# Linear attention in a fused block: all pairs of token tiles scored, or scores within a tile and states passed between tiles

## Chip, cores and metric

The kernel runs on one core of one Trainium2 chip. Its time is the device time of one execution in microseconds (us), given as the median of several runs. Engines: TensorE (PE) multiplies, VectorE (DVE) and ScalarE (ACT) do elementwise work and read PSUM, GpSimd (POOL) does elementwise work in SBUF, SyncE (SP) issues most DMAs.

## What is computed

One block of a hybrid model on 512 tokens with 1024 features: a joint input projection, a gated linear attention in two directions (4 heads, key width 128, value width 256), a softmax attention with latent keys (8 heads), their gated merge, and a squared-ReLU MLP of width 4096. The part that matters here is the linear attention. With q, k, v of a head and a log decay per token and key feature in each direction:

```python
b = jnp.cumsum(log_a, axis=3)                 # within a chunk
q_dec, k_dec = q * jnp.exp(b), k * jnp.exp(-b)
k_end = k * jnp.exp(b_last - b)
scores = jnp.where(mask, jnp.einsum('bhnck,bhnsk->bhncs', q_dec, k_dec), 0.0)
o_intra = jnp.einsum('bhncs,bhnsv->bhncv', scores, v)
def step(state, inp):                         # from chunk to chunk
    o = jnp.einsum('bhck,bhkv->bhcv', qc, state)
    state = state * dc[..., None] + jnp.einsum('bhck,bhcv->bhkv', kc, vc)
    return state, o
```

The forward direction includes a token's own key, the backward one does not; the two outputs are added, normalised per head, and gated. Everything is in float32; nearly all products are done as three "rounded" products (mm3, L87): each operand is split into a high part, rounded to the fp32r format, and the remainder, and high x high, high x low and low x high are added in PSUM. split (L92) makes the two parts: ACT copies the high one, DVE (or POOL, where given) subtracts for the low one. split_scaled (L96) does it with a scale.

## The kernel before, in words

Tokens lie in four tiles of 128. All activations are kept transposed (features on partitions, 512 tokens in the free dimension). The kernel goes through these stages: the first projections while x lands; the gates and values of the linear attention for all heads by a seven-product scheme (class Seven); the four heads of the linear attention; the softmax attention; the output projection; the MLP.

A head h of the linear attention goes through these steps, with their lines:

- Gates(h) (L435): two products for the log gates, Abs and Exp on ACT; logs (L453) takes the logarithm; sums (L456) does four scans on DVE and one subtraction per direction; exps (L472) makes from them the factors per token (ee) and per tile (e3: decay from a tile's start to its middle, from its middle to its end, and over the tile).
- gla_qk (L486): queries and keys times their factors relative to the middle of their own tile (near, on DVE), and from these on POOL a second pair for neighbouring tiles (nxt) and a third for tiles of the other half (far), each with coefficients multiplied from e3.
- gla_scores (L529): the backward scores within the tiles (bd), and for each key tile j three float32 products that together cover all 512 queries: own tile (L544), neighbour (L545), the two tiles of the other half (L546). The backward half of the diagonal block is put in by a masked copy on DVE (L550). Each [128, 512] result is split.
- gla_out (L701): for each query tile four mm3 of 256 value columns, one per key tile: 48 products.
- gla_squares (L716), gla_gated (L726), gla_turn (L733): the norm's sums on ACT and POOL, the gating on DVE, and four transpositions for each of two value halves.

Between these steps stand projections of 128 output features, each 24 products of 512 columns: za(2h) and za(2h+1) (gates of the merge), gq and gk (queries and keys of head h + 2), and in head 2 the latent projections ckv and cq instead. begin (L235 and L231) loads the 512 KB of weights into one of three staging buffers (tag wf) and splits them into one of four pairs (wh, wl); proj_run (L247) multiplies. begin_late returns the low half's subtraction as a function (lows) that is called later.

Order: PE takes the instructions in program order from the gates on up to the end of head 2 (in_program_order, L1214), ACT and DVE too (L1213). In the last head and the softmax attention a scheduler orders them by readiness and priority, with a few hand-set constraints (goes_behind, L125). PSUM has eight banks in two groups of four: "mm" for projections, gates and turns, "at" for scores and outputs. SBUF buffers are shared by size (29 of one row of 512 floats, u2; 26 of two, u4). The loop over heads 0 to 2 is at L1180; head 3 is interleaved with the latent projections and the rotary products from L1216 to L1262.

Of the kernel before, what the change touches and what calls it, by code (L numbers as in the profile page):

```python
# [18 lines left out]
P = 128  # L19
# [37 lines left out]
def tile_block(ctx: ExitStack, tc: tile.TileContext, t, out: bass.AP):  # L57
# [29 lines left out]
    def mm3(acc, lh, ll, rh, rl, start, stop, onto=False):  # L87
        nc.tensor.matmul(acc, lh, rh, start=start, stop=False, skip_group_check=onto)  # L88
        nc.tensor.matmul(acc, lh, rl, start=False, stop=False, skip_group_check=onto)  # L89
        nc.tensor.matmul(acc, ll, rh, start=False, stop=stop, skip_group_check=onto)  # L90

    def split(hi, lo, src, rest=nc.vector):  # L92
        nc.scalar.activation(hi, src, AF.Copy)  # L93
        rest.tensor_tensor(lo, src, raw(hi), op=ALU.subtract)  # L94
# [140 lines left out]
    def begin_late(col, name, tag="mm", w=None):  # L235

        wf = stage(KD, P, name)
        nc.sync.dma_start(wf, (w_in if w is None else w)[:, col : col + P].rearrange("(k p) w -> p k w", p=P))
        wh, wl = halves(KD, P, name)
        nc.scalar.activation(wh, wf, AF.Copy)  # L240

        def lows():
            nc.vector.tensor_tensor(wl, wf, raw(wh), op=ALU.subtract)

        return (wh, wl, ps(tag, name)), lows
# [237 lines left out]
            nc.scalar.activation(e3, v3, AF.Exp, scale=INV_NORM)  # L483
            self.parts[d] = ee, e3

    def gla_qk(h, parts):  # L486
        near = {}
        for d in ("f", "b"):
            near[d] = u4(f"qk{d}", F32, (P, 2, NT, P))
        for x in range(2):  # L490
            n = qk.pop((h, x))
            for d in ("f", "b"):
                nc.vector.tensor_tensor(
                    near[d][:, x].rearrange("p a b -> p (a b)"), n,
                    parts[d][0][:, x].rearrange("p a b -> p (a b)"), op=ALU.mult,
                )
        nxt = u4("qk2", F32, (P, 2, NT, P))
        far = u4("qk3", F32, (P, 2, NT, P))

        def times(dst, src, coef):  # L500
            nc.gpsimd.tensor_tensor(dst, src, coef.unsqueeze(2).to_broadcast([P, 2, P]), op=ALU.mult)

        cf = {}
        for d in ("f", "b"):
            e3 = parts[d][1]
            fq, fk = (e3[:, 0], e3[:, 1]) if d == "f" else (e3[:, 1], e3[:, 0])
            eT = e3[:, 2]
            odd, even = slice(1, 4, 2), slice(0, 4, 2)
            qs, ks = (odd, even) if d == "f" else (even, odd)
            times(nxt[:, 0, qs], near[d][:, 0, qs], fq[:, qs])  # L510
            times(nxt[:, 1, ks], near[d][:, 1, ks], fk[:, ks])
            c3 = tl([P, 2, NT], F32, "c3", 4, f"c3{d}")
            lo, hi = slice(0, 2), slice(2, 4)
            qs, ks = (hi, lo) if d == "f" else (lo, hi)
            if d == "f":
                nc.gpsimd.tensor_copy(c3[:, 0, 2:3], fq[:, 2:3])
                nc.gpsimd.tensor_tensor(c3[:, 0, 3:4], fq[:, 3:4], eT[:, 2:3], op=ALU.mult)
                nc.gpsimd.tensor_tensor(c3[:, 1, 0:1], fk[:, 0:1], eT[:, 1:2], op=ALU.mult)
                nc.gpsimd.tensor_copy(c3[:, 1, 1:2], fk[:, 1:2])
            else:  # L520
                nc.gpsimd.tensor_tensor(c3[:, 0, 0:1], fq[:, 0:1], eT[:, 1:2], op=ALU.mult)
                nc.gpsimd.tensor_copy(c3[:, 0, 1:2], fq[:, 1:2])
                nc.gpsimd.tensor_copy(c3[:, 1, 2:3], fk[:, 2:3])
                nc.gpsimd.tensor_tensor(c3[:, 1, 3:4], fk[:, 3:4], eT[:, 2:3], op=ALU.mult)
            times(far[:, 0, qs], near[d][:, 0, qs], c3[:, 0, qs])
            times(far[:, 1, ks], near[d][:, 1, ks], c3[:, 1, ks])
        return near, nxt, far

    def gla_scores(near, nxt, far):  # L529
        bd = ps("at", "bd")  # L530
        for j in range(NT):
            nc.tensor.matmul(
                bd[:, j * P : (j + 1) * P], near["b"][:, 1, j], near["b"][:, 0, j], start=True, stop=True
            )
        bds = u2("bds")
        nc.scalar.activation(bds, bd, AF.Copy)
        res = []
        for j in range(NT):
            sc = ps("at", f"sc{j}")
            dj = slice(j * P, (j + 1) * P)  # L540
            n = j + 1 if j % 2 == 0 else j - 1
            far_q = slice(2, 4) if j < 2 else slice(0, 2)
            far_c = slice(2 * P, 4 * P) if j < 2 else slice(0, 2 * P)
            nc.tensor.matmul(sc[:, dj], near["f"][:, 1, j], near["f"][:, 0, j], start=True, stop=True)  # L544
            nc.tensor.matmul(sc[:, n * P : (n + 1) * P], nxt[:, 1, j], nxt[:, 0, n], start=True, stop=True)  # L545
            nc.tensor.matmul(  # L546
                sc[:, far_c], far[:, 1, j], far[:, 0, far_q].rearrange("p a b -> p (a b)"),
                start=True, stop=True,
            )
            nc.vector.copy_predicated(sc[:, dj], after.bitcast(I32), bds[:, dj])  # L550
            hl = u4(f"sc{j}")
            split(hl[:, 0, :], hl[:, 1, :], sc)
            res.append(hl)
        return res

# [145 lines left out]
    def gla_out(h, sc):  # L701

        half, at = h // 2, (h % 2) * GDV
        accs = [ps("at", f"gla{h}o{j}") for j in range(2)]
        c = slice(at, at + GDV)
        os = []
        for i in range(NT):
            o = accs[i // 2][:, (i % 2) * GDV : (i % 2 + 1) * GDV]
            tok = slice(i * P, (i + 1) * P)
            for j in range(NT):  # L710
                mm3(o, sc[j][:, 0, tok], sc[j][:, 1, tok], v[j, half][:, 0, c], v[j, half][:, 1, c],
                    j == 0, j == NT - 1)
            os.append(o)
        return os

    def gla_squares(h, os):  # L716
        tot = sm(f"gla{h}ss")
# [373 lines left out]
    def begin_za(f):  # L1091
        return begin(C_ZA + f * P, f"za{f}")
# [74 lines left out]
    gate.exps("b")  # L1167
    gv.multiply(3)
    gv.multiply(7)
    near, nxt, far = gla_qk(0, gate.parts)  # L1170
    gv.right_split(4, 1)
    w_b = begin(C_ZB + 5 * P, "zb5")
    gv.sinks(3)
# [3 lines left out]
    w_a = begin_za(0)  # L1177
    finish_zb(5, w_b)
    ckv_, cq_ = Latent(C_CKV, 2, V_KV, "ckv"), Latent(C_CQ, 3, V_Q, "cq")
    for h in range(GH - 1):  # L1180
        sc = gla_scores(near, nxt, far)
        gate = Gates(h + 1)
        gate.logs()
        w_b = begin_za(2 * h + 1)
        acc = proj_run(w_a, xT)
        if h < 2:
            w_a, lows = begin_late(C_GQ + (h + 2) * P, f"gq{h + 2}")
        else:
            ckv_.begun[0], lows = begin_late(C_CKV, "ckv0")
        gate.sums("f")  # L1190
        gate.exps("f")
        lows()
        gate.sums("b")
        gate.exps("b")
        za_gate(2 * h, acc)
        os = gla_out(h, sc)
        near, nxt, far = gla_qk(h + 1, gate.parts)
        rs = gla_squares(h, os)
        za_gate(2 * h + 1, proj_run(w_b, xT))
        if h < 2:  # L1200
            w_b = begin_qk(h + 2, 1)
            gla_gated(h, os, rs)
            finish_qk(h + 2, 0, w_a)
            w_a = begin_za(2 * h + 2)
            finish_qk(h + 2, 1, w_b)
        else:
            ckv_.begin(1)
            gla_gated(h, os, rs)
            ckv_.run(0)
            cq_.begin(0)  # L1210
            ckv_.run(1)
        gla_turn(h)
# [17 lines left out]
    cq_.sums()  # L1230
    zb = proj_T(C_ZB + 6 * P, "zb6")
    projected = traced()
    sc = gla_scores(near, nxt, far)
# [5 lines left out]
    goes_behind((at, traced()), (projected, scored), PE_ONLY)  # L1239
    spreading = traced()  # L1240
    cq = cq_.normed()
    goes_behind((spreading, traced()), (projected, scored), PE_ONLY)
# [10 lines left out]
    for _ in range(3):  # L1253
        next(units)
    at = traced()
    os = gla_out(h, sc)
    values = traced()
    for _ in units:
        pass
# [413 lines left out]
```

## Time and profile before

| | us |
|---|---|
| median of 3 runs | 766.08 |
| lowest, highest | 764.56, 766.45 |
| span of the profiled execution, first to last instruction | 764.1 |
| stretch of heads 0, 1, 2 (PE starts of the scores or turns: 144.69, 177.36, 210.76, 244.17) | 32.7, 33.4, 33.4 |
| PE busy in 144.69 to 244.17 | all of it |
| DVE, ACT, POOL busy in 177.36 to 210.76 | 21.4, 19.4, 13.0 |

The profiled execution has no time of its own beside its span; the runs' times include some 2 us around the span. The profile gives, for each instruction, its engine, its line in the kernel, its start and duration, and what ended the idle time before it. Matmul durations overlap, so the distance of their starts is what one costs in a row. Where a helper such as mm3 or split records the operation, the line is the helper's (L88 to L90, L93, L94) and the tile's name tells what it is: sc for scores, gla0o for the output of head 0, za, gq, gk for projections. PEld is the load of the stationary operand, which runs beside the matmuls.

### The profile page before, as it was taken

The numbers are of one execution on the slowest core, as the hardware profiler recorded it, in microseconds if no ns is written. First come the engines' busy times: TensorE is split into PE (matmuls) and PEld (weight loads), VectorE is DVE, ScalarE is ACT, GpSimd is POOL, SyncE is SP. The second block draws the span as 40 slices with busy tenths as digits, with TensorE's granted clock in tenths as the row PEclk, the third lists the DMA queues.
The fourth block names the chain that finished last, engine by engine and source line by source line (L and its number), as shares of the span: only waits on it lengthen the run. The fifth ranks groups of instructions, "written<-read, shape, count | busy, mean of one in ns | idle before, by whom it ended". The sixth has DMA issues, their size and how long they took to land.

```text
span 764.1 us, 10232 instructions
## 1 busy us (share of the span) xinstructions
PE 754.0 (99%) x3744; PEld 637.5 (83%) x3744; DVE 580.7 (76%) x851; ACT 453.1 (59%) x768; POOL 151.1 (20%) x226
## 2 busy tenths in 40 slices
PE   8999999999999999999999999999999999999996
PEld 7888788888898888899888988888888888888885
DVE  7689999765667865898897886965787578748795
ACT  7556658384566555888866775435653555346634
POOL 1630004351605104117762100000000000000014
PEclk9999999999999999999999999999999999999999
DMA  9832411222323516127989421363116410650002
GB/s 317 248 88 88 135 28 28 56 56 56 83 55 91 102 37 155 25 60 187 258 200 242 138 83 55 111 190 86 55 56 190 140 36 21 194 164 1 27 1 110
DMA packets 97073, 81.28 MB, mean 106 GB/s; under 512 B 15376, under 2 KB 74784, under 8 KB 97024
## 3 DMA queue, kind: packets, MB, share of 16 engines
q1 hardware_dynamic: 93760, 74.07, 33.0%
q0 software_dynamic: 2976, 6.05, 4.3%
q8 instruction: 29, 0.48, 0.3%
q10 hardware_dynamic: 288, 0.52, 0.2%
q14 instruction: 20, 0.16, 0.1%
HBM read 76.96 MB, written 2.10 MB: 103 GB/s over the span
## 4 chain that ended last, share of the span: by engine, by line
PE 96%; DVE 1%; ACT 1%; DMA 1%; issue 0%; POOL 0%; POOLq 0%; ACTq 0%
PE f L88 8%; PE f L90 8%; PE f L89 8%; PE gx L88 4%; PE gx L89 4%; PE gx L90 4%; PE first L329 3%; PE tp L1046 2%; PE za L88 2%; PE za L89 2%; PE za L90 2%; PE gz L90 2%; PE gz L88 2%; PE gz L89 2%; PE zb L88 1%; PE zb L89 1%
## 5 line engine op out<-in xcount | busy, mean ns | idle before, releaser
L1612 POOL DMA_DIRECT2D gfin<-in_g_final x1 | 0.6, 622 | 284.0 <-PE f L90 284.0
L918 DVE TENSOR_TENSOR w<-w,w 128x1024 f32<-128x1024 f32 x32 | 38.8, 1223 | 0.3
L479 POOL COPY v3f<-rrf 128x4 f32<-128x4 f32 x4 | 2.8, 707 | 136.0 <-DVE rrf L462 136.0
L1031 ACT ACTIVATE e<-s,top 128x512 f32<-128x512 f32 x32 | 21.9, 685 | 4.7 <-DVE top L1026 3.8
L94 DVE TENSOR_TENSOR pT<-tp,pT 128x512 fp32r<-128x512 f32 x32 | 21.7, 683 | 3.0 <-ACT pT L93 3.0
L1026 DVE TENSOR_REDUCE top<-s 128x1 f32<-128x512 f32 x32 | 21.7, 683 | 2.0 <-PE s L90 1.7
L1339 DVE TENSOR_TENSOR h<-h,gx 128x512 f32<-128x512 f32 x32 | 21.5, 684 | 1.9 <-PE gx L90 1.8
L93 ACT ACTIVATE pT<-tp 128x512 fp32r<-128x512 f32 x32 | 18.8, 592 | 4.3 <-PE tp L1046 4.0
L1046 PE MATMUL tp<-ident,e 128*128 128x128 f32 x128 | 19.3, 274 | 0.4 <-ACT e L1037 0.2
L88 PE MATMUL av<-pT,v 128*128 128x256 f32 x64 | 19.0, 297 | 0.0
L1405 ACT ACTIVATE fa<-f 128x512 f32<-128x512 f32 x32 | 18.5, 577 | 0.0
L93 ACT ACTIVATE ghb<-y 128x512 fp32r<-128x512 f32 x16 | 10.1, 632 | 14.0 <-DVE y L864 14.0
L89 PE MATMUL av<-pT,v 128*128 128x256 f32 x64 | 18.2, 285 | 0.0
L90 PE MATMUL av<-pT,v 128*128 128x256 f32 x64 | 18.2, 284 | 0.0
L1046 PEld LDWEIGHTS tp<-ident,e 128*128 128x128 f32 x128 | 15.1, 140 | 3.7 <-ACT e L1037 1.0
L94 DVE TENSOR_TENSOR sc<-sc,sc 128x512 fp32r<-128x512 f32 x16 | 10.9, 691 | 9.5 <-ACT sc L93 9.5
L93 ACT ACTIVATE sc<-sc 128x512 fp32r<-128x512 f32 x16 | 9.3, 595 | 11.5 <-DVE sc L550 11.5
L93 ACT ACTIVATE b_00h<-w 128x1024 fp32r<-128x1024 f32 x7 | 7.4, 1059 | 12.5 <-PE gx L90 6.0
L93 ACT ACTIVATE b_10h<-w 128x1024 fp32r<-128x1024 f32 x7 | 7.4, 1060 | 12.1 <-PE gx L90 6.0
L93 ACT ACTIVATE b_20h<-w 128x1024 fp32r<-128x1024 f32 x7 | 7.4, 1060 | 12.1 <-PE gx L90 6.0
L88 PE MATMUL s<-kbuf,q 96*128 96x512 f32 x32 | 14.1, 441 | 0.0
L1414 ACT ACTIVATE px<-fa 128x256 f32<-128x256 f32 x32 | 13.4, 418 | 1.0
(1668 smaller groups left out, 2932.2 us busy)
## 6 DMA issues: line engine op xcount, KB each, us to landing
w<-in_w_ff SPq DMA_DIRECT2D x64, 256.0 KB, 3.4
w<-in_w_out POOLq DMA_DIRECT2D x10, 512.0 KB, 9.4
grw<-in_w_in SPq DMA_DIRECT2D x8, 512.0 KB, 9.0
gvw<-in_w_in SPq DMA_DIRECT2D x8, 512.0 KB, 4.9
w<-in_w_out SPq DMA_DIRECT2D x16, 256.0 KB, 5.5
x<-in_xt SPq DMA_DIRECT2D x8, 256.0 KB, 5.3
h<-in_x SPq DMA_DIRECT2D x4, 512.0 KB, 5.0
vw<-in_w_first SPq DMA_DIRECT2D x7, 256.0 KB, 5.4
```

What stands on the lines that cost most here:

```text
L88: nc.tensor.matmul(acc, lh, rh, start=start, stop=False, skip_group_check=onto)
L89: nc.tensor.matmul(acc, lh, rl, start=False, stop=False, skip_group_check=onto)
L90: nc.tensor.matmul(acc, ll, rh, start=False, stop=stop, skip_group_check=onto)
L93: nc.scalar.activation(hi, src, AF.Copy)
L94: rest.tensor_tensor(lo, src, raw(hi), op=ALU.subtract)
L329: nc.tensor.matmul(f_accs[i], a[:, i * P : (i + 1) * P], b, start=k == 0 and x == 0, stop=k == KD - 1 and x == 2)
L918: nc.vector.tensor_tensor(wq[dst][g], wq[x][g], wq[y][g], op=op)
L1026: nc.vector.tensor_reduce(top, acc, axis=AX.X, op=ALU.max, negate=True)
L1031: nc.scalar.activation(e, acc, AF.Exp, bias=top, accum_out=tot[:, qt % 2 : qt % 2 + 1])
L1046: nc.tensor.transpose(tp[:, k * P : (k + 1) * P], e[:, k * P : (k + 1) * P], ident)
L1339: nc.vector.tensor_tensor(hc, hc, acc, op=op)
L1405: nc.scalar.activation(a, acc, AF.Relu)
```

## The change

Scores are now only taken within a tile of 128 tokens, both directions. For what lies in other tiles, every tile passes on a state (keys times values, 128 x 256) per direction. near is as before, keys first. The class Linear then has these steps:

- turned: six float32 transpositions bring the keys of the three tiles that pass something on, per direction, into token-major form; split.
- queries: the near queries of the three receiving tiles are split, the low half on POOL.
- scores: eight float32 128x128 products, one masked copy per tile, one split.
- values: for each of three levels and two directions one mm3, transposed keys by values, 18 products in three PSUM banks.
- states: per direction a running sum over the levels, scaled by the decays (coefs are made on POOL from e3), every level split into high (ACT) and low (DVE).
- out: for each query tile one mm3 on its scores and one on each state that it receives: (4 + 6) x 3 = 30 products.

The loop is rearranged: za(1) and Gates(1) come ahead of head 0, Gates(h + 2) between the gq and gk projections of head h; the order in a head is turned, queries, scores, za(2h), values, states, sums, za(2h + 1), out, gating, gq(h + 2), gates, gk(h + 2), turn. In head 3 turned to scores stand where the scores stood, values behind za6, out where it was. gla_qk, gla_scores and gla_out are gone.

```diff
-    def gla_qk(h, parts):
...
-        nxt = u4("qk2", F32, (P, 2, NT, P))
-        far = u4("qk3", F32, (P, 2, NT, P))
...
-    def gla_scores(near, nxt, far):
...
+    class Linear:
...
+        def turned(self):
+            self.kt = {}
+            for d, src in (("f", FWD), ("b", BWD)):
+                bank = ps("at", f"kt{d}")
+                for n, j in enumerate(src):
+                    nc.tensor.transpose(bank[:, n * P : (n + 1) * P], self.near[d][:, 1, j], ident)
+                hl = u4(f"kt{d}")
+                split(hl[:, 0, 0:C3], hl[:, 1, 0:C3], bank[:, 0:C3])
+                self.kt[d] = hl
+
+        def queries(self):
...
+                split(hl[:, 0, 0:C3], hl[:, 1, 0:C3], src, nc.gpsimd)
...
+        def scores(self):
...
+                for j in range(NT):
+                    nc.tensor.matmul(
+                        banks[d][:, j * P : (j + 1) * P], self.near[d][:, 1, j], self.near[d][:, 0, j],
+                        start=True, stop=True,
+                    )
...
+        def values(self):
+            banks = [ps("at", f"kv{n}") for n in range(3)]
...
+                    mm3(acc, k[:, 0, tok], k[:, 1, tok], vt[:, 0, self.cols], vt[:, 1, self.cols], True, True)
...
+        def states(self, coefs):
...
+            for d, src in order:
+                nc.scalar.activation(held[d][:, 0], self.kv[d, 0], AF.Copy, scale=coefs[d][:, 1:2])
+            highs(0, each(lambda d, src: self.kv[d, 0]), each(lambda d, src: coefs[d][:, 0:1]))
+            for n in (1, 2):
+                for d, src in order:
+                    u, j = held[d][:, n - 1], src[n]
+                    nc.vector.scalar_tensor_tensor(u, self.kv[d, n], fk[d][:, j : j + 1], u, op0=ALU.mult, op1=ALU.add)
+                    if n == 1:
+                        m = src[2]
+                        nc.scalar.activation(held[d][:, 1], u, AF.Copy, scale=eT[d][:, m : m + 1])
+                lows(n - 1)
+                to = each(lambda d, src: src[n] + (1 if d == "f" else -1))
+                highs(n, each(lambda d, src: held[d][:, n - 1]), each(lambda d, src: fq[d][:, to[d] : to[d] + 1]))
+            lows(2)
+
+        def out(self):
...
+                terms = [(self.sc[:, 0, tok], self.sc[:, 1, tok], vt[:, 0, c], vt[:, 1, c])]
+                for d, n in (("f", i - 1), ("b", i)):
+                    if (d, i) in self.s:
+                        q, st = self.q[d], self.s[d, i]
+                        at = slice(n * P, (n + 1) * P)
+                        terms.append((q[:, 0, at], q[:, 1, at], st[:, 0], st[:, 1]))
+                for n, term in enumerate(terms):
+                    mm3(o, *term, n == 0, n == len(terms) - 1)
...
     for h in range(GH - 1):
-        sc = gla_scores(near, nxt, far)
-        gate = Gates(h + 1)
-        gate.logs()
-        w_b = begin_za(2 * h + 1)
+        lin.turned()
+        lin.queries()
+        lin.scores()
+        if h:
+            w_b = begin_za(2 * h + 1)
         acc = proj_run(w_a, xT)
...
+        lin.values()
+        lin.states(coefs)
         gate.sums("f")
...
+        past, acc = acc, proj_run(w_b, xT)
+        os = lin.out()
+        rs = gla_squares(h, os)
...
+        lin = Linear(h + 1, gate.parts, gla_near(h + 1, gate.parts))
+        coefs = gla_coefs(gate.parts)
...
             finish_qk(h + 2, 0, w_a)
+            gate = Gates(h + 2)
+            gate.logs()
             w_a = begin_za(2 * h + 2)
-            finish_qk(h + 2, 1, w_b)
+            finish_qk(h + 2, 1, w_k)
```

Here highs(n, ...) makes the high parts of level n's states on ACT, lows(n) the low parts on DVE.

More of the change, by code (lines that the diff above doesn't have):

```diff
@@ L484, in exps, with gla_near @@
             self.parts[d] = ee, e3
-    def gla_qk(h, parts):
[L487 to L490, printed above, removed]
+    FWD, BWD = (0, 1, 2), (3, 2, 1)
+    def gla_near(h, parts):
+        near = {d: u4(f"qk{d}", F32, (P, 2, NT, P)) for d in ("f", "b")}
+        for x in (1, 0):
             n = qk.pop((h, x))
@@ L496, in gla_qk @@
                 )
-        nxt = u4("qk2", F32, (P, 2, NT, P))
-        far = u4("qk3", F32, (P, 2, NT, P))
[L500 to L526, printed above, removed]
@@ L527, in gla_qk @@
-        return near, nxt, far
-    def gla_scores(near, nxt, far):
[L530 to L533, printed above, removed]
-            )
[L535 to L548, printed above, removed]
-            )
[L550 to L554, printed above, removed]
@@ new lines, in gla_near, with decays, gla_coefs @@
+        return near
+    def decays(d, e3):
+        fq, fk = (e3[:, 0], e3[:, 1]) if d == "f" else (e3[:, 1], e3[:, 0])
+        return fq, fk, e3[:, 2]
+    def gla_coefs(parts):
+        coefs = {}
+        for d, src in (("f", FWD), ("b", BWD)):
+            fq, fk, eT = decays(d, parts[d][1])
+            c = tl([P, 2], F32, "c3", 4, f"c3{d}")
+            first, second = src[0], src[1]
+            nc.gpsimd.tensor_tensor(
+                c[:, 0:1], fq[:, second : second + 1], fk[:, first : first + 1], op=ALU.mult
+            )
+            nc.gpsimd.tensor_tensor(
+                c[:, 1:2], eT[:, second : second + 1], fk[:, first : first + 1], op=ALU.mult
+            )
+            coefs[d] = c
+        return coefs
@@ L699, in za_gate @@
         za_gates[f] = z
[L701 to L714, printed above, removed]
     def gla_squares(h, os):
@@ L1169, in tile_block @@
     gv.multiply(7)
-    near, nxt, far = gla_qk(0, gate.parts)
+    lin = Linear(0, gate.parts, gla_near(0, gate.parts))
+    coefs = gla_coefs(gate.parts)
     gv.right_split(4, 1)
@@ L1232, in tile_block @@
     projected = traced()
-    sc = gla_scores(near, nxt, far)
+    lin.turned()
+    lin.queries()
+    lin.scores()
     scored = traced()
@@ L1239, in tile_block @@
     goes_behind((at, traced()), (projected, scored), PE_ONLY)
+    valued = traced()
+    lin.values()
+    goes_behind((valued, traced()), (at, valued), PE_ONLY)
+    lin.states(coefs)
     spreading = traced()
@@ L1255, in tile_block @@
     at = traced()
-    os = gla_out(h, sc)
+    os = lin.out()
     values = traced()
```

89 lines of the change are left out of this document (76 added, 13 removed).

## The prediction, made before the changed kernel ran

> **What bounds the kernel now.** I read the page first: its span, the busy shares (part 1) and the chain that ended last (part 4).
>
> ```profile
> span 764.1 us, 10232 instructions
> PE 754.0 (99%) x3744; PEld 637.5 (83%) x3744; DVE 580.7 (76%) x851; ACT 453.1 (59%) x768; POOL 151.1 (20%) x226
> ...
> PE 96%; DVE 1%; ACT 1%; DMA 1%; issue 0%; POOL 0%; POOLq 0%; ACTq 0%
> ```
>
> TensorE (PE) is busy for 99% of the span and 96% of the last chain is its own instructions. The waits of PE, by whom it waited for, are the second view:
>
> ```profile
> PE first L329 <- ACT xT L97: 1.5, 1, 1.5
> PE warm L319 <- DVE ones L145: 1.1, 1, 1.1
> PE grx L88 <- DVE grc L667: 0.4, 1, 0.4
> PE tp L1046 <- ACT e L1037: 0.2, 1, 0.2
> ```
>
> None of these lies between 144 and 307 us, where the four heads of linear attention run. So that stretch is a queue of matmuls with nothing between them: a matmul that disappears there is worth its pace, and a wait put in there costs its length. The other engines matter only where they make PE wait. The median of the runs (766.08 us) stands 2.0 us above the profiled span, which I take for what lies around it; the sum below is made on the span and the 2.0 us are added again at the end.
>
> **What PE does for one head.** "Busy" counts matmuls that overlap, so I take paces from starts in the PE timeline (columns: start, duration, engine, line, operation):
>
> ```profile
> 144.69 1.05 PE L532 MATMUL bd<-qkb 128*128 128x128 f32 x8
> ...
> 149.56 0.39 PE L88 MATMUL za<-xT,za0h 128*128 128x512 f32 x1
> ...
> 155.00 0.28 PE L88 MATMUL gla0o<-gv,sc 128*128 128x256 f32 x1
> 155.12 0.28 PE L89 MATMUL gla0o<-gv,sc 128*128 128x256 f32 x1
> ...
> 160.76 0.40 PE L88 MATMUL za<-xT,za1h 128*128 128x512 f32 x1
> ...
> 177.36 0.38 PE L741 MATMUL y<-ident,gra 128*128 128x128 f32 x2
> ...
> 178.23 1.06 PE L532 MATMUL bd<-qkb 128*128 128x128 f32 x8
> 179.13 0.39 PE L544 MATMUL sc<-qkf 128*128 128x128 f32 x2
> ...
> 180.01 0.38 PE L544 MATMUL sc<-qkf 128*128 128x128 f32 x2
> ...
> 182.46 0.58 PE L445 MATMUL gatef<-z,gate_f 128*128 128x512 f32 x1
> 182.87 0.40 PE L445 MATMUL gateb<-z,gate_b 128*128 128x512 f32 x1
> 183.11 0.39 PE L88 MATMUL za<-xT,za2h 128*128 128x512 f32 x1
> ...
> 210.76 0.38 PE L741 MATMUL y<-ident,gra 128*128 128x128 f32 x2
> ```
>
> - A float32 128x128 product (two records) keeps the pace 0.90 / 4 = 0.225 us (bd, 178.23 to 179.13). One key tile of scores (128, 128 and 256 columns) takes 180.01 - 179.13 = 0.88. bd and four such tiles run from 178.23 to 182.46, and the first gate product behind them takes 0.41 where the second takes 0.24, so 0.17 of their tail belongs to them: 4.40 us.
> - The 48 rounded products of 256 columns take 160.76 - 155.00 = 5.76 us, 0.12 each.
> - A transposition takes (178.23 - 177.36) / 8 = 0.109.
> - A projection (24 products of 512 columns) takes 155.00 - 149.56 = 5.44, the two gate products 0.45.
>
> **The change on PE.** It removes bd and the four score tiles (4.40) and all 48 value products (5.76): 10.16 us a head. It adds six transpositions (0.65), eight float32 score products of 128 columns (8 x 0.225 = 1.80), 18 products for the states (3 x 2 groups of three, 2.16) and 30 for the output (12 within tiles, 18 against states, 3.60): 8.21 us. The rounded products are 48 in both; what goes is the nxt and far scores, less the transpositions. **Saved: 1.95 us a head, 7.8 us in four.** The order of the projections around it changes, not their number; after the last head PE's order is the same as before, and so is the MLP.
>
> [...]
>
> **What it adds to ACT, DVE and POOL.** Scores split by ACT and DVE shrink from four tiles to one; added are two splits of transposed keys (384 columns), two of queries (low halves on POOL), and the states: ten ACT copies and ten DVE operations of 256 columns. The eight POOL products per head go. None of this bounds by its sum; the question is what PE now waits for: kv (values) waits for the split keys, and out (Linear.out) waits for the last state, whose chain goes kv, scaled copy (ACT), add (DVE), copy (ACT), low half (DVE), three levels deep. Behind the waiting output stand all later matmuls. Prices:
>
> ```profile
> 145.68 0.63 ACT L374 ACTIVATE tb<-zb 128x512 f32<-128x512 f32 x1 [4.59 <-DVE zb L372]
> 146.21 0.58 ACT L536 ACTIVATE bds<-bd 128x512 f32<-128x512 f32 x1
> ...
> 152.34 0.68 ACT L446 ACTIVATE l<-gatef,gvec 128x512 f32<-128x512 f32 x1
> ...
> 156.96 1.04 ACT L93 ACTIVATE za1h<-za1f 128x1024 fp32r<-128x1024 f32 x1
> 157.91 1.05 ACT L240 ACTIVATE gq2h<-gq2f 128x1024 fp32r<-128x1024 f32 x1
> ...
> 269.21 0.52 ACT L93 ACTIVATE wr0h<-wr0f 128x384 fp32r<-128x384 f32 x1 [3.70 <-PE zb L89]
> ```
> ```profile
> 158.04 1.23 DVE L94 TENSOR_TENSOR za1l<-za1f,za1h 128x1024 fp32r<-128x1024 f32 x1 [3.55 <-ACT za1h L93]
> 159.18 1.37 DVE L462 TENSOR_TENSOR_SCAN rrf<-mf,l 128x128 f32<-128x128 f32 x4
> ...
> 174.96 0.88 DVE L731 SCALAR_TENSOR_TENSOR gra<-gla0o,gla0ss,gra 128x256 f32<-128x256 f32 x2 [2.77 <-POOL gla0ss L723]
> ```
>
> An ACT operation of 1024 columns keeps the pace 0.95; the gate's work on ACT (two Abs, Exp, table load, Ln) takes 156.96 - 152.34 = 4.62; 384 columns take 0.52, pace some 0.45 (estimate); a DVE operation of 1024 columns 1.14, four dependent ones of 128 columns 1.37, and one of 256 columns from PSUM 0.88 - 0.48 = 0.40 in pace and 0.48 to its end (estimate, the pair split).
>
> **Head 0** is the tight one, since Gates(1) and za1 are moved ahead of it. ACT and DVE keep program order there. From the rows: zb5 leaves PE at 144.69; ACT is free at 146.21, then za1h 0.95 and the gate 4.62, so the first key split starts at 151.78. Four 384-column copies end the queue at 153.6, bds (0.6) at 154.2, four masked copies on DVE (1.37) at 155.6, the score split's high half (0.6) at 156.2, gq2h (0.95, it stands ahead of the states on ACT) at 157.1, its low half on DVE (1.14) at 158.25, and then ten DVE operations of the states at 0.40 and the last one's tail: 162.35. PE: 144.69 + gates 0.45 + transpositions 0.65 + scores 1.80 + za0 5.44 gives 153.03 for kv (the split keys are there by about 153.3, the second group waits for them, the loss is some 0.1; kv's three PSUM banks are those of the keys and of the backward scores, free by 154.2), + 2.16 + za1 5.44 gives 160.6 for out, which does three products on the scores (0.36) and then needs the state of the last level: 160.97. **Wait: 1.4 us.**
>
> **Heads 1 and 2.** The gate stands a whole projection earlier, so ACT and DVE are through with the next weights (gq3, ckv0) when kv begins, at K. The first add can start at K + 0.72 + 0.36 + 0.2 = K + 1.3, the states end at K + 5.4, and out asks at K + 2.16 + 5.44 + 0.36 = K + 8.0: 2.6 us to spare. I cost them at nothing; the cover is the projection za3 or za5. Their weights are loaded earlier than now, behind buffers that come free sooner.
>
> **Head 3.** Between kv and out lie za7, zb7, the rotary products, uq and uk, over 18 us, so the states are free. But their DVE work is put between cqrs and the split of the normed cq, for which the rotary products wait, and the third split's high half stands behind wq0h, which waits for za7:
>
> ```profile
> 279.95 1.87 DVE L777 TENSOR_TENSOR cqc<-cqc,cqrs 128x512 f32<-128x512 f32 x3
> ...
> 282.21 1.89 DVE L94 TENSOR_TENSOR cqhl<-cqc,cqhl 128x512 fp32r<-128x512 f32 x3
> ...
> 286.03 0.95 DVE L838 TENSOR_SCALAR krsin<-sin,gvec 32x512 f32<-32x512 f32 x1
> ```
>
> Behind cqrs DVE has 1.87 + eight state operations 3.2 + za7 0.7 + krsin 0.95 + 1.89 = 8.6 us; PE reaches the first rotary product 5.44 + 2.04 (nine of zb7) + 0.48 = 8.0 us behind the start of cqrs, and needs the third split 1.4 us later. It is even; I put 0.2 us.
>
> Small gain: now the gk projections wait for their low halves, which the new order makes earlier.
>
> ```profile
>   DVE gk2l L94: 0.4, 1
>   DVE gk3l L94: 0.2, 1
> ```
>
> I take half of that, 0.3 us (the first part of such a wait is overlap of matmuls); next late there is the PSUM bank that gk takes over from za, free some 2 us before by the same reckoning. **Sum: -7.8 - 0.3 + 0.1 + 1.4 + 0.2 = -6.4. 764.1 - 6.4 + 2.0 = 759.7 us.** Own range: head 0 between no wait (758.3) and twice the wait (761.1).
>
> **Rivals.**
> - *The states are slower than their rows.* DVE beside POOL is slowed in this kernel:
>
> ```profile
> 134.15 1.63 DVE L94 TENSOR_TENSOR gv41l<-gvw,gv41h 128x1024 fp32r<-128x1024 f32 x1
> ```
>
> against 1.23 for za1l, a factor of 1.33. In head 0 POOL does the query low halves between about 153 and 155. If everything there on DVE and the chain itself went at 1.33, the masked copies, gq2l and the ten operations (6.6 us) would cost 2.2 more; with the rotary wait of head 3 at 1 us, 762.7. Against it: POOL is through before the states start. [...]
> - *Transpositions do not overlap behind each other*: 6 x (0.27 - 0.109) x 4 = 3.9 us lost, 763.6. The y rows speak against it.
> - *The gain stops at attention.* From head 3's out on PE needs scores whose q parts come from the rotary products through DMA, and those are not earlier. The copies of q and the first score product now:
>
> ```profile
> 294.98 3.92 SPq L989 DMA_DIRECT2D q<-ro  x4
> ```
> ```profile
> q<-ro SPq DMA_DIRECT2D x12, 64.0 KB, 2.4
> ```
> ```profile
> 306.66 0.40 PE L88 MATMUL s<-kbuf,q 96*128 96x512 f32 x1
> ```
>
> If that binds, head 3's 1.95 us and 0.3 more are lost: 762. But the copies land at 294.98 + 3.92 + 2.4 = 301.3, 5.4 us before their use, and 3.4 of that are left.
> - *Slower: ACT stands before a load.* gq(h+2) and ckv0, split on ACT ahead of the state chain, come by DMA; now ACT does wait for loads at such places (zb6h 3.06, za6h 2.08):
>
> ```profile
> 248.61 1.06 ACT L93 ACTIVATE zb6h<-zb6f 128x1024 fp32r<-128x1024 f32 x1 [3.06 <-DMA zb6f<-in_w_in]
> 251.75 1.06 ACT L93 ACTIVATE za6h<-za6f 128x1024 fp32r<-128x1024 f32 x1 [2.08 <-DMA za6f<-in_w_in]
> ```
>
> A load d late costs d in head 0 and d - 2.6 in heads 1 and 2; 3d - 5.2 reaches the 6.4 us at d = 3.9, and at d = 5 it is 769.5. Against it: each of these loads is issued when a staging buffer comes free, by the reckoning above some 15 us before its use (gq3: at the end of gk2's low half).
> - *That the change does not do what it says* is excluded on PE: 36 fewer matmul instructions stand in its order, in the places named.
>
> **How the numbers follow.** Forecast 759.7 (758.3 to 761.1): 0.62. Better, since head 0 waits for nothing and paces are a little under the rows: 0.07. States slow or gain stopped, 761.1 to 763.6: 0.18. Transpositions in sequence, 763.6 and a little more: 0.03. Several of these, up to 768: 0.05. Load late, slower: 0.05. 0.3% of 766.08 is 2.3 us, about what a measurement of this kernel can tell from no change: faster is below 763.8, slower above 768.4. Faster 0.87, same 0.08, slower 0.05. The range 757.5 to 763.6 leaves out 0.05 on the low side and 0.13 on the high one.
>
> **What would show it.** Each head's period on PE (y to y, now 33.40 us from 177.36 to 210.76) shrinks to 31.4 in heads 1 and 2; head 0 shows one wait of 1 to 2 us at its first state product, on DVE's last low half; kt and kv keep the paces 0.109 and 0.12; ro waits under 0.5. It would be wrong if the out products wait in heads 1 and 2, or the stretch from head 3's out to the end is not the same length as before.

## The result and the profile after

| | before | after |
|---|---|---|
| median of the runs made side by side, us | 765.37 (764.56 to 766.45) | 758.86 (758.09 to 759.76) |
| span of the profiled execution, us | 764.1 | 756.5 |

The ratio after to before is 0.9918, 95% interval 0.9903 to 0.9933: 6.5 us less, where 6.4 were forecast. In a second set of runs on another occasion the same kernel stood at 759.29 against 765.93, ratio 0.9914 (0.9900 to 0.9927). Two executions, one of the kernel before in this second set and one of the kernel with four idle operations below, took 944 and 933 us at a granted clock of 0.75; the ratios leave them out, the medians 765.93 and 766.83 count them (765.90 and 766.54 without).

The page of the changed kernel, the lines that answer to those shown of before:

```profile
span 756.5 us, 10217 instructions
...
PE 745.2 (99%) x3704; PEld 629.7 (83%) x3704; DVE 592.5 (78%) x887; ACT 468.1 (62%) x812; POOL 128.1 (17%) x186
...
PE 93%; ACT 2%; DVE 2%; issue 1%; DMA 1%; POOL 0%; POOLq 0%; ACTq 0%; DVEq 0%
```

PE has 40 records less (per head 32 of the old float32 scores against 16 of the new and 6 transpositions; the prediction's 36 counted runs of equal instructions as one) and 8.8 us less of busy time; DVE and ACT have more to do, POOL less. On the last chain, ACT and DVE now hold 2% each: some stretch of their work sets the end. The waits of PE say which. Their columns are whom it waited for, the total, the times, the longest:

```profile
PE first L329 <- ACT xT L97: 1.3, 1, 1.3
...
PE gla0o L88 <- ACT st L598: 0.6, 1, 0.6
PE gla0o L89 <- DVE st L591: 0.6, 1, 0.6
```

New is gla0o, the output of head 0, on the high half of a state (ACT) and then on its low half (DVE). There is none in heads 1, 2 and 3. The PE timeline (start, duration, engine, line, operation) at the bounds of the stages:

```profile
143.62 0.39 PE L445 MATMUL gatef<-z,gate_f 128*128 128x512 f32 x1
...
144.07 0.49 PE L533 MATMUL ktf<-ident,qkf 128*128 128x128 f32 x3
...
144.73 1.06 PE L551 MATMUL scb<-qkb 128*128 128x128 f32 x8
145.62 1.06 PE L551 MATMUL scf<-qkf 128*128 128x128 f32 x8
146.43 0.47 PE L88 MATMUL za<-xT,za0h 128*128 128x512 f32 x1
...
151.99 0.28 PE L88 MATMUL kv<-gv,ktf 128*128 128x256 f32 x1
...
154.14 0.40 PE L88 MATMUL za<-xT,za1h 128*128 128x512 f32 x1
...
159.61 0.28 PE L88 MATMUL gla0o<-gv,sc 128*128 128x256 f32 x1
...
160.76 0.39 PE L88 MATMUL gla0o<-st,qsb 128*128 128x256 f32 x1 [0.64 <-ACT st L598]
161.74 0.39 PE L89 MATMUL gla0o<-st,qsb 128*128 128x256 f32 x1 [0.59 <-DVE st L591]
...
164.96 0.40 PE L88 MATMUL gq<-xT,gq2h 128*128 128x512 f32 x1
...
176.32 0.38 PE L811 MATMUL y<-ident,gra 128*128 128x128 f32 x2
...
207.68 0.38 PE L811 MATMUL y<-ident,gra 128*128 128x128 f32 x2
...
238.59 0.38 PE L811 MATMUL y<-ident,grb 128*128 128x128 f32 x2
...
299.00 0.40 PE L88 MATMUL s<-kbuf,q 96*128 96x512 f32 x1
```

| stretch on PE, us | before | after | difference |
|---|---|---|---|
| start to head 0 (bd; gatef) | 144.69 | 143.62 | -1.07 |
| head 0, to its turn | 32.67 | 32.70 | +0.03 |
| head 1, turn to turn | 33.40 | 31.36 | -2.04 |
| head 2, turn to turn | 33.41 | 30.91 | -2.50 |
| head 3 and up to the first attention score | 62.49 | 60.41 | -2.08 |
| from there to the end of the span | 457.44 | 457.5 | 0 |

Two pairs of gate products (0.45 us) now stand in head 0's stretch and none in head 2's; without this shift the differences are -0.42, -2.04, -2.05 and -2.08, together -6.6. The first row is no gain of the change: the changed kernel was at 144.81 at this point in another profile. So three heads give what the products are worth, and head 0 gives back 1.75 us: its 30 products take 164.96 - 159.61 = 5.35, where 30 x 0.12 is 3.60. (The two waits of the view, 1.2 us, are less than the loss: the view counts a wait from the end of the product before, 0.28 to 0.39 us behind its start, while in a row the next product starts after 0.12.)

The chain behind that wait, in the ACT, DVE and POOL timelines of head 0:

```profile
150.70 0.47 ACT L93 ACTIVATE ktf<-ktf 128x384 fp32r<-128x384 f32 x1
...
152.27 0.60 ACT L556 ACTIVATE bds<-scb 128x512 f32<-128x512 f32 x1
154.94 0.60 ACT L93 ACTIVATE sc<-scf 128x512 fp32r<-128x512 f32 x1 [2.07 <-DVE scf L559]
155.44 1.05 ACT L93 ACTIVATE gq2h<-gq2f 128x1024 fp32r<-128x1024 f32 x1
```
```profile
152.90 2.01 DVE L559 COPY_PREDICATED scf<-after,bds 128x128 f32<-128x128 int32 x4 [0.67 <-ACT bds L556]
155.57 0.69 DVE L94 TENSOR_TENSOR sc<-scf,sc 128x512 fp32r<-128x512 f32 x1 [0.66 <-ACT sc L93]
156.52 1.23 DVE L94 TENSOR_TENSOR gq2l<-gq2f,gq2h 128x1024 fp32r<-128x1024 f32 x1 [0.26 <-ACT gq2h L93]
157.66 0.48 DVE L613 SCALAR_TENSOR_TENSOR wf<-kv,e3f,wf 128x256 f32<-128x256 f32 x1
...
161.20 0.48 DVE L591 SCALAR_TENSOR_TENSOR st<-wb,e3b,st 128x256 fp32r<-128x256 f32 x1
```
```profile
152.04 1.02 POOL L94 TENSOR_TENSOR qsf<-qkf,qsf 128x384 fp32r<-128x384 f32 x1 [24.37 <-ACT qsf L93]
153.02 1.06 POOL L94 TENSOR_TENSOR qsb<-qkb,qsb 128x384 fp32r<-128x384 f32 x1
```

Key split, the two copies of the queries, backward copy, masked copies, high half of the scores, gq2, ten state operations at 0.39: every link starts where the one before ends, and the last low half ends at 161.68. PE asked for it at 159.97. The masked copies took 2.01 us, while POOL made the query low halves beside them. It is one of the four that is long, the second:

```profile
153.25 0.98 DVE L559 COPY_PREDICATED scf<-after,bds 128x128 f32<-128x128 int32 x1
```

It ends 0.15 behind the second POOL subtraction; the other three took 0.30 to 0.32.

### The profile page after: what moved, and what is told of

Its sections match the earlier page's. It is cut to its first block, busy times and chain, and to the rows that moved or that the text cites. A ratio compares the mean times of both kernels' runs of the same rounds, so it can differ in the third digit from the quotient of the medians.

```text
span 756.5 us, 10217 instructions
## 1 busy us (share of the span) xinstructions
PE 745.2 (99%) x3704; PEld 629.7 (83%) x3704; DVE 592.5 (78%) x887; ACT 468.1 (62%) x812; POOL 128.1 (17%) x186
## 4 chain that ended last, share of the span: by engine, by line
PE 93%; ACT 2%; DVE 2%; issue 1%; DMA 1%; POOL 0%; POOLq 0%; ACTq 0%; DVEq 0%
PE f L89 8%; PE f L88 8%; PE f L90 8%; PE gx L88 4%; PE gx L89 4%; PE gx L90 4%; PE first L329 3%; PE tp L1116 2%; PE gz L89 2%; PE gz L88 2%; PE gz L90 2%; PE zb L88 1%; PE za L88 1%; PE zb L90 1%; PE za L90 1%; PE za L89 1%
## 5 line engine op out<-in xcount | busy, mean ns | idle before, releaser
L374 ACT ACTIVATE tb<-zb 128x512 f32<-128x512 f32 x8 | 5.0, 632 | 14.7 <-DVE zb L372 14.7
L984 POOL DMA_DIRECT2D w<-in_w_out x10 | 12.2, 1397 | 6.5 <-DVE bo60l L94 5.3
```

## Experiments

Theory: PE's queue sets the time, so products count by their pace; the wait of head 0 is the end of the ACT and DVE chain, and heads 1 to 3 have their states in time because a projection lies between values and output. Rivals: the new order of the loop gives the gain, or PE is not what bounds. "Head 0" is from its first gate product to its turn, heads 1 and 2 from turn to turn, all PE starts; the changed kernel has 32.70, 31.36 and 30.91.

### The within-tile scores issued twice

```diff
-                for j in range(NT):
+                for j in 2 * list(range(NT)):
                     nc.tensor.matmul(
```

> The eight float32 128x128 score products of Linear.scores are issued twice, in all four heads; the second set overwrites the first with the same values, nothing else changes. Theory A (the time of these heads is the sum of PE's paces, and what the change gains is the paces of the products that went): eight more products at 0.225 us are 1.80 us a head. In heads 1, 2 and 3 PE has no wait, so each is 1.8 us longer. In head 0 the keys' splits, the masked copies and the states run from ACT's and DVE's own queue: scf ends 1.8 later, at about 148.2, still ahead of its masked copies (first at 152.9), so the last state is no later and the 1.75 us wait of the first output product takes the whole of it: head 0 +0 to +0.1. Together +5.4 us: 758.9 + 5.4 = 764.3. Rival B (the gain comes from the order of the loop, PE merely looks busy): under +1 us, 759 to 760. Rival C (every PE product counts, also in head 0): +7.2, 766.1.

Measured: 765.08 us, ratio 0.9986 (0.9977 to 0.9995). Head 0 32.74, head 1 33.14, head 2 32.70, head 3's stretch 62.24: +0.04, +1.78, +1.79, +1.83. (The median is 6.2 above the changed kernel's 758.86, but the kernel before stood higher in this set too, at 766.31 and not 765.37; by the ratios it is 0.0068, 5.2 us.) Theory A holds in each head: a product costs its pace where PE does not wait, and nothing where it waits for something that the product does not hold up.

### The old scores in the new order

The class Linear out, the old three functions in, called at the places of the new loop (gla_scores where turned to scores stand, gla_out where out stands).

> The old functions (scores over all pairs of tiles, 48 value products) in the new order of the loop: za1 and the gate of head 1 ahead of head 0, the gate of head h + 2 between gq and gk, both projections ahead of the output. Theory A (the gain is the paces of the products that went): nothing is gained in heads 1 to 3 but the waits on the low halves of gk2 and gk3 (0.6 us in the trace of before), and head 0 has its scores behind the gate and the splits of za1 on ACT, which it has two projections (10.9 us) to take up: 764.5 to 766, with 765 the likeliest. Rival B (the order gives the gain): 759 to 761. Periods from turn to turn in heads 1 and 2: 33.3 by A, 31.4 by B.

Measured: 774.11 us, ratio 1.0110 (1.0095 to 1.0124); head 0 38.32, heads 1 and 2 35.12 and 34.31. Rival B falls, but theory A's number was 9 us off: this order makes the old scores slower than they were. The waits of PE in this kernel:

```profile
PE sc L544 <- ACT bds L536: 3.6, 1, 3.6
...
PE za L88 <- ACT za3h L93: 0.7, 1, 0.7
PE za L90 <- DVE za3l L94: 0.5, 1, 0.5
PE za L90 <- DVE za5l L94: 0.5, 1, 0.5
...
PE za L88 <- ACT za5h L93: 0.4, 1, 0.4
```

In head 0 the first three score tiles fill their PSUM banks and the fourth waits for the backward copy, which stands on ACT behind za1's split and the gate; behind that wait the granted clock falls as well (0.70, 0.50, 0.50 and 0.59 in the four microseconds from 152.0, which makes some 3.4 us at 0.50), as in the experiment with idle operations. I had looked only at what the output waits for. In heads 1 and 2 the weights of the second projection are split behind four score splits instead of one.

### The new scores in the old order

```diff
-    w_b = begin_za(1)
-    gate = Gates(1)
-    gate.logs()
     for h in range(GH - 1):
         lin.turned()
         lin.queries()
         lin.scores()
+        gate = Gates(h + 1)
+        gate.logs()
+        w_b = begin_za(2 * h + 1)
         acc = proj_run(w_a, xT)
         lin.values()
         lin.states(coefs)
...
         za_gate(2 * h, acc)
         os = lin.out()
...
         za_gate(2 * h + 1, proj_run(w_b, xT))
```

> The other half of the change alone: the class Linear in the loop of before (gate of h + 1 and the split of za(2h + 1) behind the scores, values and states behind za(2h), the output right behind them, za(2h + 1) last). Theory (PE needs a projection between values and output to cover the states): ACT reaches the first state copy some 10.2 us from the first turn, behind key and query splits 1.6, backward copy 0.6, score split 0.6 after the masked copies, the gate's 4.6 and za's 0.95; ten DVE operations at 0.39 and the level's steps end some 5 us behind that, at 15.2, and PE asks at 10.9: a wait of 4.3 in each of heads 0 to 2, against 1.75 in head 0 alone. Heads 1 and 2 take 31.4 + 4.3 = 35.7 us, time 758.9 - 1.75 + 12.9 = 770 (767 to 773), slower than the kernel before. Rival (the products alone give the gain, in any order): heads at 31.4 to 32, 758 to 760.

Measured: 778.94 us, ratio 1.0169 (1.0153 to 1.0184); heads 1 and 2 take 38.12 and 37.91. The direction was right, the size was not: the output of head 1 takes 10.37 us, a loss of 6.8 where 4.3 were expected. The waits of PE:

```profile
PE gla0o L88 <- ACT st L598: 5.2, 1, 5.2
PE gla1o L88 <- ACT st L598: 4.2, 1, 4.2
PE gla2o L88 <- ACT st L598: 4.2, 1, 4.2
```

In head 1 the last low half ends 16.1 us behind the first turn instead of 15.2 (the masked copies took 2.01 here too, and the first add stands behind za3's low half on DVE); the other 1.5 us are a fall of the granted clock behind the wait (0.61 from 200.0 to 202.0, 0.54 from there to 204.0), as in the next experiment. The outputs of heads 0 and 2 take 11.91 and 10.17, losses of 8.3 and 6.6. The three losses in place of the one of 1.75 make 758.86 - 1.75 + 21.7 = 778.8 us, beside the 778.94 measured: they are the whole difference. So each half of the change alone loses, 7.8 us and 12.7 us by the medians, and both together gain 6.5.

### Idle DVE operations ahead of the states, heads 1 and 2

```diff
         lin.values()
+        if h:
+            idle = u4("idle", F32, (P, 2, NT, P))
+            for _ in range(4):
+                nc.vector.tensor_tensor(
+                    idle.rearrange("p x a b -> p (x a b)"), lin.near["f"].rearrange("p x a b -> p (x a b)"),
+                    lin.near["f"].rearrange("p x a b -> p (x a b)"), op=ALU.add,
+                )
         lin.states(coefs)
```

One such operation, then four.

> One idle DVE addition of 1024 columns (1.14 us in pace) ahead of the ten state operations, in heads 1 and 2. In the changed kernel DVE works without a gap there (low halves of two weights, then the ten operations at 0.39), and its last low half ends 2.0 us before PE asks for it (191.10 against 193.08 in head 1, 222.46 against 224.44 in head 2). Theory (spare time of 2.0 us): nothing, both heads keep 31.36 and 30.91 us, time unchanged within 0.3. Rival (DVE is on the path in these heads as in head 0, PE's 99% hides it): +1.1 each, +2.3 in all.

> Four such additions (4.56 us) in heads 1 and 2. Theory (2.0 us to spare, from there one to one): each head waits 2.56 us in its output, 33.9 and 33.5 us, +5.1 us, time 764.0. Rival A (more to spare than 2.0, since the states' order can give): under +3. Rival B (DVE on the path from the start): +9.1.

Measured with one: 759.55 us beside 759.29 of the changed kernel, heads 31.36 and 30.91: nothing, as the theory had it. With four: 766.83 us, ratio to before 1.0009 (0.9999 to 1.0018), heads 35.84 and 33.87: +4.48 and +2.96, where 2.56 each were expected. The operations ran at 1.23, not 1.14, so the last state is 4.91 - 2.0 = 2.9 late: that is head 2. Head 1 waited as long and lost 1.5 more. Windows of its trace (bounds; PE busy, PEld, DVE, ACT, POOL, PEclk, DMA), head 1 in three rows and head 2 in two:

```profile
193.00:196.00 3.00, 0.72 (x4) 0.32 (x3) 3.00 (x8) 3.00 (x7) 0.00 (x0) 1.00 0.00 0
196.00:199.50 3.50, 3.31 (x15) 3.32 (x16) 3.43 (x11) 0.69 (x4) 1.42 (x5) 0.54 0.00 0
199.50:202.00 2.50, 2.50 (x17) 2.33 (x17) 2.50 (x4) 1.10 (x7) 1.08 (x4) 0.96 0.00 0
...
229.00:232.00 3.00, 0.57 (x3) 0.19 (x1) 3.00 (x9) 2.91 (x6) 0.00 (x0) 1.00 0.00 0
232.00:235.00 3.00, 2.98 (x25) 2.98 (x26) 2.97 (x9) 0.84 (x4) 1.29 (x3) 1.00 0.00 0
```

After the wait of head 1 PE had a mean granted clock of 0.54 over 3.5 us, and its products of 256 columns stand 0.213 apart, not 0.12; sixteen of them make the 1.5 us. After the same wait in head 2 the clock stays 1.00.

### The splits of gq2 behind the states, head 0

```diff
-        if h < 2:
+        if h == 1:
             w_a = begin_qk(h + 2, 0)
-        else:
+        elif h == 2:
             ckv_.begin(0)
         lin.values()
         lin.states(coefs)
+        if h == 0:
+            w_a = begin_qk(h + 2, 0)
```

> In head 0 alone the split of the gq weights of head 2 (ACT copy 0.95, DVE subtraction 1.14) is put behind the state operations instead of ahead of them. My theory: the 1.75 us wait of head 0's output on the last low half is the end of a chain of ACT and DVE in program order, in which gq2 is a link: the first state copies move up by ACT's 0.95, the adds by DVE's 1.14 or to where kv is ready (kv starts at 151.99, its last group ends about 154.2), so the last low half ends 0.9 to 1.2 earlier, at 160.5 to 160.8 instead of 161.68, and the wait shrinks from 1.75 to 0.6 to 0.9. gq2 is needed at 164.96 less the wait, when its splits are through at about 163.5. Time 758.9 - 1.0 = 757.9. Rival (the chain of the states themselves sets the end, from kv's end, at their pace): the wait stays 1.5 or more, 758.6 to 758.9. Worse rival: gq2 is now late for its projection, 759 to 760.

Measured: 758.20 us, ratio 0.9898 (0.9882 to 0.9914). Head 0 takes 31.36, 1.34 less; its output 4.00, a loss of 0.4. gq2 is a link of the chain, a little more than expected (0.9 to 1.2), and its projection does not wait. The rival that the states' own pace sets the end falls.

### The queries behind the scores

```diff
         lin.turned()
-        lin.queries()
         lin.scores()
+        lin.queries()
```

> The splits of the queries (two ACT copies of 384 columns, 0.42 each in pace, low halves on POOL) stand behind the split of the scores instead of ahead of it, in all four heads. In the trace of the changed kernel the four masked copies of head 0 took 2.01 us, where they took 1.29 in heads 1 and 2, and the two POOL low halves ran beside them (152.04 to 154.08). Theory: beside POOL such a copy is slowed, and bds stands 0.84 later on ACT than it need. Without both, the scores' backward copy starts at 151.44, the masked copies end about 1.5 us earlier, and the chain behind them (high half, gq2h, ten state operations) up to that, less the 0.84 that ACT then does for the queries ahead of gq2h: the last low half 0.7 to 1.5 earlier, wait 0.3 to 1.1 instead of 1.75, time 757.4 to 758.2. If POOL's low halves slow DVE wherever they stand (next: the low halves of the scores and of gq2), the gain is 0 to 0.5: 758.4 to 758.9. Masked copies: 1.3 us if contention with POOL was their cost, 2.0 if it was something else (the end of bds, for instance).

Measured: 759.73 us, ratio 0.9917 (0.9905 to 0.9930); head 0 32.56, only 0.14 less. The DVE timeline:

```profile
153.89 1.29 DVE L559 COPY_PREDICATED scf<-after,bds 128x128 f32<-128x128 int32 x4
...
157.62 1.75 DVE L94 TENSOR_TENSOR gq2l<-gq2f,gq2h 128x1024 fp32r<-128x1024 f32 x1 [1.08 <-ACT gq2h L93]
```

The masked copies are back at 1.29, so POOL beside them was their cost. But POOL's low halves now run from 156.30 to 158.29, and gq2's low half pays 0.52 in their place; ACT's two copies are only moved within the chain. The theory's gain fell, the rival's reading (POOL's low halves slow DVE at their next place too) was right for gq2's low half: 1.75 where it took 1.23.

### The queries where ACT and POOL are idle, then both moves

ACT idles 4.59 us ahead of its work on zb5 (to 144.60). Head 0's queries go there:

```diff
     w_a = begin_za(0)
+    lin.queries()
     finish_zb(5, w_b)
...
         lin.turned()
-        lin.queries()
+        if h:
+            lin.queries()
         lin.scores()
```

> Only the first of the two moves: head 0's queries are split ahead of zb5's turn, in ACT's and POOL's idle time; gq2's split stays ahead of the states. Where the queries stood behind the split of the scores, the masked copies went from 2.01 to 1.29 but gq2's low half, then beside POOL, from 1.23 to 1.75, and ACT's 0.84 were only moved. Theory: put where neither DVE nor ACT has work, the 0.72 and the 0.84 are both gained: the last low half of head 0 ends 1.5 earlier (160.2 on the clock of the changed kernel), the wait is 0.2 to 0.4 instead of 1.75, head 0 takes 31.2 to 31.4 from the gates to the turn, time 1.4 less than the changed kernel, 757.5. Rival (the ACT copies were no link, only POOL's contention): the gain is 0.7, head 0 in 32.0, 758.2.

Measured: 757.90 us, ratio 0.9889 (0.9873 to 0.9906); head 0 31.24, loss in its output 0.29. As forecast: the last low half ends 1.46 us earlier, where the two links together were 0.72 + 0.84 = 1.56 long.

With gq2's move added, and the changed kernel beside it on the same chip:

> The changed kernel without any edit, beside the next one on the same chip. Both theories: 0.992 of the kernel before (0.990 to 0.993), 32.7 us from the gates to the turn of head 0, with 1.7 us of wait in its output.

> Head 0 alone, two moves. The splits of its queries go ahead of zb5's turn, where the trace of the changed kernel shows ACT idle for 4.59 us (to 144.60) and POOL for over 20 us; and gq2's split goes behind the states. My theory (the wait in head 0's output is the end of a chain on ACT and DVE, whose links are the two query copies of 0.42, the four masked copies that take 2.01 beside POOL's query low halves and 1.29 without them, and gq2's low half of 1.14): without the links the last low half ends about 2.6 us earlier than 161.68, at 159.1 to 159.6, before PE asks for it at 159.97. The wait goes: 1.75 us less, head 0 in 30.9 us from the gates to the turn, time 0.9895 of before, 757.1 to 757.3 where the changed kernel is at 758.9. Rival (POOL's two low halves must slow something on DVE wherever they stand, or the early buffers hold up another split): 0.3 to 0.5 us of wait left, head 0 in 31.4, as with gq2 moved alone.

Measured: 756.96 us, ratio to before 0.9882 (0.9868 to 0.9895), against 759.29 of the changed kernel, whose head 0 took 32.70 again. This version beats both kernels: the runs of the two do not overlap (756.48 to 757.47 and 759.23 to 759.80). Its DVE and PE timelines:

```profile
152.10 1.29 DVE L559 COPY_PREDICATED scf<-after,bds 128x128 f32<-128x128 int32 x4
...
158.34 0.48 DVE L591 SCALAR_TENSOR_TENSOR st<-wb,e3b,st 128x256 fp32r<-128x256 f32 x1
```
```profile
159.56 0.28 PE L88 MATMUL gla0o<-gv,sc 128*128 128x256 f32 x1
...
163.15 0.40 PE L88 MATMUL gq<-xT,gq2h 128*128 128x512 f32 x1
```

The last low half ends at 158.82, before the output starts; the 30 products take 3.59 and PE has no wait left in the four heads. Head 0 is 30.94, 1.76 less: the whole of the 1.75.

## Why the prediction was right, point by point

- **PE sets the time.** Shown by the doubled scores: +1.8 in every head without a wait, +0.04 in head 0.
- **8.21 us added on PE per head.** In the PE timeline kt takes 144.73 - 144.07 = 0.66, the scores 1.70 (forecast 1.80; 0.1 of their tail is in the projection behind), kv 2.15, the output 3.59 where it does not wait. The saving of 1.95 came out at 1.91 to 1.94 in heads 0 to 2, if head 0's wait and the waits on low halves (below) are taken out, and at 2.08 in head 3. Head 3's 0.2 for the rotary products is not there: ro took 4.08 us, as before.
- **Transpositions.** Three in 0.33 us, 0.109 each. The rival's 0.27 is the duration of one transposition's record (L741 in before: 270 to 273 ns), not what one costs in a row here; that rival fell.
- **Head 0, 1.4 us.** Measured 1.75: the mechanism and the place were those named (DVE's last low half of the states). Counted from the first gate product, the key split started at 7.08 (forecast 7.09), PE asked at 16.35 (16.28), and the last low half ended at 18.06 (17.66). The mis-sized term is the four masked copies, 1.37 in the sum and 2.01 in the trace; ACT's four copies, 0.25 shorter than taken, give some of it back. The rival "states slower" had the cause right, POOL beside DVE, but not its place: POOL was through at 154.08, and the ten state operations kept their 0.39. A masked copy took 0.98 beside POOL and 0.30 without. The prediction's rule that a wait costs its length held here (1.71 between asking and the last low half, 1.75 lost); it did not hold for longer waits of the experiments, behind which the granted clock fell to 0.50 (head 1 with four idle operations: 2.9 late, 4.48 lost).
- **Heads 1 and 2 without a wait.** Right; 2.0 us to spare, not 2.6. DVE's low halves of the next weights end later than I took them to, as its timeline of head 1 in the changed kernel shows (PE asks at 193.08):

```profile
185.95 1.22 DVE L94 TENSOR_TENSOR gq3l<-gq3f,gq3h 128x1024 fp32r<-128x1024 f32 x1
...
190.62 0.48 DVE L591 SCALAR_TENSOR_TENSOR st<-wb,e3b,st 128x256 fp32r<-128x256 f32 x1
```

  One idle operation there costs nothing, four cost 2.9 and more.
- **The gk waits, 0.3.** gk took 5.70 and 5.55 us in heads 0 and 1 of before and takes 5.44 in both now; ckv1, the projection at that place in head 2, went from 5.56 to 5.45 in the same way, which the sum had left out: 0.48 together.
- **The gain stops at attention; a load comes late.** Neither: from the first attention score to the end nothing changed, and ACT waits for no load in front of the states.

The errors cancel: 0.35 more in head 0, against 0.2 that did not come in head 3, 0.2 more at the waits on low halves, 0.1 that did not come at kv, and 0.1 more from the products. That the difference came within 0.1 us of the sum is in part luck; no single term was off by more than 0.35. The time itself lies 0.8 under the 759.7, since the kernel before stood at 765.37 in the runs made side by side and not at 766.08.

## What to carry to other kernels

When a change shortens the queue of the bounding engine and puts a dependent chain on two others, write that chain down link by link in queue order: what is not part of it but stands in its queue (here a weight split) is where the loss sits, and moving it behind the chain, or to where its own engines are idle, gives it back. Products and order belong together: the smaller scores need a projection between values and output (778.94 us without it), and that order by itself makes the larger scores wait (774.11 us). A stall on a busy PE can cost more than its length (4.48 us for 2.9 in head 1 with four idle operations), so leave room ahead of it rather than just enough.

## What the runs showed of the hardware

- A 128x128 masked copy took 0.28 to 0.30 us alone and up to 0.98 beside a POOL subtraction in SBUF; a low half of 1024 columns went from 1.23 to 1.75. POOL pays as well: the first query low half took 1.64 beside DVE's za0 low half in the last version, 1.02 in the changed kernel. In these rows the extra time goes by what the other engine's operation still had to run when this one began: 0.68 of 0.83 for the copy, 0.52 of 0.67 for the low half, 0.62 of 0.77 for POOL, and 0.40 of 0.56 for gv41's low half in the kernel before, from which the prediction took its factor of 1.33. Each time it is some 0.15 us less, and no one factor covers them (3.3, 1.42, 1.61 and 1.33). Not every row of before goes by it: in its POOL timeline the product at 134.67 took 1.59 where others took 1.06, 0.53 more, with 1.11 of gv41's low half still to run. What holds the operations up no run was made to test.
- With four idle operations, after a wait of 2.0 us, one product and a wait of 0.6, the granted clock fell to 0.50 in head 1, and after the same waits in head 2 it stayed at 1.00. In head 1 it was 0.50 in every half microsecond from 196.5 to 199.5, 0.77 in the one before and 0.82 in the one behind: some 3.4 us at 0.50 in all. With waits of 4.2 to 5.2 us it fell to 0.50 in all three heads of the new scores in the old order (for 3.4 us in heads 1 and 2; for 6.8 in head 0, where it fell before the wait was over), and after the 3.6 us in head 0 of the old scores in the new one. The wait of head 0 in the changed kernel (0.6, one product, 0.6) left it at 1.00. PE's idle share alone does not tell the two heads apart: it was busy for 0.72 of the 3 us from 193.00, behind which the clock fell, and for 0.57 of the 3 us from 229.00, behind which it did not. What decides it no run shows.
